# An encoder block with attention and a two-way scan: banks for the scan's copies, an earlier join, and a new order at the start

## The chip, the cores and the metric

The kernel runs on one core of a Trainium2 chip. The metric is device time in microseconds, as the median of several runs: 866.34 us before the change (three runs, 866.20 to 866.93). A profile is one execution of the program, taken on the same core.

The engines are TensorE (PE, with its weight loads as PEld), VectorE (DVE), ScalarE (ACT), GpSimd (POOL) and SyncE (SP). SP issues almost all loads.

## The reference

One layer over 256 tokens of 2048 channels, all in float32. Cut to what matters:

```
h    = rms_norm(x, g_pre)
proj = h @ w_in                        # 2048 x 10688: q_a, kv_a, k_rope | r, k, v, low ranks | z | gates
# branch 1: latent attention, 8 heads
q  = rms_norm(q_a) @ wq_b;  kv = rms_norm(kv_a) @ wkv_b
y1 = softmax((q_nope k_nope + rot(q_rope) rot(k_rope)) * 192**-0.5) v
# branch 2: RWKV-7 in both directions, 16 heads of 64
r, k, v, wd, ad = mix(rin)             # with the mean of both neighbour tokens
w = exp(-exp(-softplus(-(w0 + tanh(wd) @ w2)) - 0.5));  a = sigmoid(a0 + ad @ a2)
kk = k * k_k, normalised per head
for each token:  S = S*w + (S @ -kk) (kk*a)^T + v k^T;   y = S @ r      # forward and backward
y2 = group_norm(y) + bonus * v
merged = sigmoid(g1) * ((y1*silu(z1)) @ w_br_mla) + sigmoid(g2) * ((y2*silu(z2)) @ w_br_rwkv)
x = x + rms_norm(merged @ w_out, g_post)
```

## The kernel before, in words

**Order.** All instructions are written by a planner in Python. Each piece of work is a generator, a stream, that asks for an engine with a cost in us (`yield ("P", 0.48, ready)`), waits for a condition (`"W"`) or for a time (`"T"`). `Streams.run` picks for each engine the stream that can start first, and among near ones the one of lowest rank. Only this choice depends on the costs: the result is one fixed queue per engine, run in order, with semaphores between them. `O.add(stream, rank)` starts a stream. A wrong cost makes a queue whose instructions wait longer than planned.

**Projections.** Weights come in chunks of 4 blocks of 128 channels by 256 columns (`dma_stream`, three raw buffers). `split_stream` splits each into a high part (ScalarE, L331) and a low part (VectorE, L334), and `cm_task` multiplies (L400 to L402): three products per block, high by high, high by low, low by high. These products are the bulk of TensorE's work and fill its queue between all other pieces. Results go to three PSUM banks `d`; all small work uses five banks `m` (`MB`), each 512 float32 wide. `MB.take()` waits for a free one.

**Start.** x arrives in five loads. TensorE transposes the first half of x unscaled (`turned`, tiles `u`) and runs the first half of the low-rank projection on it, to be scaled afterwards (`ev_first`, with the row `R` of 1/rms that `spread` makes: two diagonal tiles on VectorE, four products, one ScalarE copy). `row(t)` sums the squares of token tile t, ScalarE for t = 0 (L1425) and VectorE for t = 1 (L1428), both into one scratch tile `junk`; then comes 1/rms (L1431 to L1435) and the scaling of x (L1442, L1446). The scaled x is transposed again (L1464) and evicted as a high part `hhi` (L1452) and a low part `hlo`, sixteen tiles, k = 8 to 15 first. `start` itself makes derived vectors (`vd`, `ka1`, L1499 to L1503) that `mix` uses as scales.

**RWKV, in quarters.** Four quarters Q of four heads each, and both directions: eight head-directions. `front_k`, `front_d`, `front_v` and `bonus` prepare a quarter, `chunks_of(Q)` does the scan in four chunks of 64 tokens. It makes Gram matrices for all 8 x 4 = 32 chunks (L801), turns the 32 x 32 blocks with VectorE's transposes (L823, L824), inverts 64 triangular blocks of 32 with 60 small VectorE instructions, turns back (L851 to L855), and joins two blocks of 32 to one of 64: two rounds (L856) of 32 small products and four copies (L872), which alternate between ScalarE and VectorE out of one bank. Then the four steps in order (L900): `pu` holds the right-hand sides of all eight head-directions in one bank `mu`, one half of the heads on partitions 0 to 63 and the other on 64 to 127. ScalarE copies one half, VectorE the other (L921, L923); a product with the inverse follows (L928), two copies again (L930, L932), then the products for the next state and the output (L946, L949). The next quarter's preparation starts when `z.u8_free` is set, after the join, and so lies beside the scan. `head_sums` adds over the 64 channels of a head by a product with a block-diagonal matrix `bdr`, from a high and a low part; it is called four times in a quarter.

**Afterwards** come the attention's projections and heads, the two branch projections, and the output projection (L1333 to L1335, 512 columns each).

Of the kernel before, what the change touches and what calls it, by code (L numbers as in the profile page):

```python
# [26 lines left out]
S0 = 1.5  # L27
# [131 lines left out]
def encoder_block_kernel(  # L159
# [117 lines left out]
    def dma_stream():  # L277
        i = 0

        before = {0: [("x", 0, 1)], 1: [("kr", 0, 2)], 2: [("x", 1, 1)], 3: [("kr", 2, 6), ("x", 2, 2)],  # L280
                  5: [("x", 4, 2), ("x", 6, 2)], 6: [("kr", 8, 8)]}
        O.free["S"] = S0
        while True:
            for what, k, n in before.get(i, ()):
                if what == "x":
                    e = yield ("S", 0.73 * n, 0.0)
                    C = slice(256 * k, 256 * (k + n))
                    nc.sync.dma_start(xt[:, :, C], xv[:, :, C])
                    for kp in range(k, k + n):
                        have["xl", kp] = e  # L290
                else:
                    have["kr", k] = yield ("S", 0.182 * n, 0.0)
                    o = krw[k // 8][:, 0:512].rearrange("p (k c) -> p k c", k=8)
                    nc.sync.dma_start(o[:, k % 8:k % 8 + n], w_in_v[:, k:k + n, 1024:1088])
            yield ("W", lambda: i < len(chunks) and i < done["split"] + NRAW)
            c = chunks[i]
            c.t = yield ("S", 0.55 if i < 2 else 1.1 if i < 9 else 1.46, O.free["D"] if i > 9 else 0.0)
            c.load(raws[i % NRAW])
            i += 1
            if i == 8:  # L300
                for t, src in ((rope, rope_d), (bdone, bdone_d), (mask, mask_d), (works[-1], scanm_d)):
                    nc.sync.dma_start(t, src)
            done["dma"] = i
# [117 lines left out]
    def mix(p, m, mcol, o):  # L421

        q = yield from QP.take()
        for j in range(2):
            yield ("A", cA(256, 1))
            act.activation(q[0:m, j, 1:257], p[0:m, j], AF.Copy, scale=vd[0:m, mcol + j:mcol + j + 1])
        t = yield from W.take()
        tv = w2d(t)
        yield ("D", cD(512))
        tt(tv[0:m], q[0:m, :, 0:256], q[0:m, :, 2:258], ALU.add)  # L430
        QP.give(q)
        for j in range(2):
            yield ("D", cD(256))
            stt(o[0:m, j], p[0:m, j], vec[0:m, mcol + j:mcol + j + 1], tv[0:m, j], ALU.mult, ALU.add)
        W.give(t)
# [149 lines left out]
    def head_sums(v, m):  # L585

        n, (hi, lo) = yield from take_r()
        yield from two_parts(v, w2d(hi), w2d(lo))
        yield ("P", 0.476)
        for j in range(2):  # L590
            pe.matmul(p2(m)[:, j], bdr, w2d(hi)[:, j], start=j == 0, stop=False)
            pe.matmul(p2(m)[:, j], bdr, w2d(lo)[:, j], start=False, stop=j == 1)
        give_r(n)
# [69 lines left out]
    def front_d(Q, d):  # L663
# [37 lines left out]
        yield ("D", cD(520))  # L701
# [69 lines left out]
    def chunks_of(Q):  # L771
# [19 lines left out]

        for d in range(2):
# [29 lines left out]
        yield ("D", 4.1)  # L822
        dve.transpose(out=Af[B1], in_=Gu[B1, :, 0:32].rearrange("p u t -> p t u"))  # L823
        dve.transpose(out=Af[B2], in_=Gu[B2, :, 32:64].rearrange("p u t -> p t u"))  # L824
# [4 lines left out]
        yield ("A", cA(1024))  # L829
        act.copy(Af[Lo], Af[Hs])  # L830
        e1 = yield ("D", cD2(512), O.free["D"])
        dve.tensor_copy(Tc[Hs], Ae[Hs, :, 1])
        e0 = yield ("A", cA(512))
# [16 lines left out]
        yield ("D", 2.0)  # L850
        dve.transpose(out=tm[B1].rearrange("p u s -> p s u"), in_=Ai[B1].rearrange("p t s -> p s t"))  # L851
        yield ("D", 2.0)
# [3 lines left out]
        for step in range(2):  # L856

            m = yield from MB.take()
            pm = m[:, 0:256].rearrange("p (u c) -> p u c", u=8)
            e = yield ("P", 0.5, None, "32x32")  # L860
            for u in range(32):
                j = 32 * (u % 4)
                o = pm[j:j + 32, u // 4]
                if step == 0:
                    pe.matmul(o, Gu[B1, u, 32:64], tm[B1, u], start=u < 4, stop=u >= 28, tile_position=(64, j))
                else:
                    pe.matmul(o, tm[B2, u], Gu[B2, u, 32:64], start=u < 4, stop=u >= 28, tile_position=(96, j))
            for j in range(4):
                on, cost = (("A", cA(256) + 0.07), ("D", cD(256) + 0.09))[j % 2]
                yield (on, cost, e)  # L870
                copy = act.copy if on == "A" else dve.tensor_copy
                copy(tm[B2, j::4] if step == 0 else Gu[B1, j::4, 32:64], pm[32 * j:32 * j + 32])  # L872
            MB.give(m)
            yield ("T", max(O.free["A"], O.free["D"]))
# [18 lines left out]
        def by_v(pu, q):  # L893

            for dj in range(4):
                for h in range(2):
                    pe.matmul(pu[R64[1 - h], dj], G[:, 2 * dj + h, q, 0:64], z.uv[q][:, 2 * dj + h], start=dj == 0,
                              stop=(dj == 3 and q == 0))

        for q in range(4):  # L900
# [3 lines left out]
            if q == 0:  # L904
                mu = yield from MB.take()
                pu = mu[:, 0:256].rearrange("p (a c) -> p a c", a=4)
                e = yield ("P", 0.48, None, "128x64")
                by_v(pu, q)
            m = yield from MB.take()
            py = m[:, 0:256].rearrange("p (a c) -> p a c", a=4)  # L910
            if q:
                e = yield ("P", 0.5, None, "64x64")

                for dj in range(4):
                    ar = z.ar[dj // 2][:, dj % 2, q]
                    for h in range(2):
                        pe.matmul(pu[R64[1 - h], dj], ar[R64[h], 0:64], Z[R64[h], dj], start=False, stop=dj == 3)
                    for h in range(2):
                        pe.matmul(py[R64[h], dj], Z[R64[h], dj], ar[R64[h], 64:128], start=dj == 0, stop=False)
            e0 = yield ("A", cA(256) + 0.08, e)  # L920
            act.copy(rhs[Hs, 1], pu[R64[0]])  # L921
            e1 = yield ("D", cD(256) + 0.11, e)
            dve.tensor_copy(rhs[Hs, 0], pu[Hs])  # L923
            e = yield ("P", 0.48, max(e0, e1), "64x64")
            for a in range(4):
                for i in range(2):
                    st = 4 * i + a
                    pe.matmul(pu[R64[i], a], G[Hs, st, q, 0:64], rhs[Hs, st % 2, st // 2], start=a == 0, stop=a == 3)  # L928
            e1 = yield ("A", cA(256) + 0.08, e)
            act.copy(uv[Hs, 0:4], pu[R64[0]])  # L930
            e2 = yield ("D", cD(256) + 0.11, e)
            dve.tensor_copy(uv[Hs, 4:8], pu[Hs])  # L932
            MB.give(mu)
# [4 lines left out]
            mu = (yield from MB.take()) if q < 3 else None  # L938
# [11 lines left out]
            if q < 3:  # L950
                pu = mu[:, 0:256].rearrange("p (a c) -> p a c", a=4)
# [450 lines left out]
    def start():  # L1402
        junk = sb([128, 4, 512], "b8", 1)
# [14 lines left out]
        def row(t):  # L1418
            e = []
# [76 lines left out]
        O.add(spread(), 1)  # L1496
        yield ("W", lambda: ("rs", 1) in have)

# [4 lines left out]
        ts(vd[:, V_KK:V_KK + 8], vec[:, V_KK:V_KK + 8], -1.0, 0.0)  # L1503
        yield ("W", lambda: done["dma"] >= 8)
# [148 lines left out]
```

## Time and profile before

| | before |
|---|---|
| median of three runs | 866.34 us |
| the profiled execution's own time | 866.99 us |
| its span | 865.2 us |
| instructions | 19404 |
| PE busy | 843.4 us (97%) |
| DVE busy | 660.1 us (76%) |
| ACT busy | 501.0 us (58%) |
| POOL busy | 31.8 us (4%) |
| DMA | 139.41 MB, mean 161 GB/s |

The span runs from the first to the last recorded instruction; the execution's own time is a little longer. Matmuls are pipelined: the time shown for one runs over into the next, so how fast products follow one another is read from their starts. A wait is given with the engine and line that ended it.

### The profile page before, as it was taken

What the parts mean: (1) busy time and instruction counts of PE and PEld (TensorE: products, weight loads), DVE (VectorE), ACT (ScalarE), POOL (GpSimd) and SP (SyncE); (2) the same over time, 40 slices, a digit from 0 to 9 for tenths busy, and PEclk for the clock granted to TensorE, in tenths of its full rate; (3) what the DMA queues carried; (4) which work ended last, traced back from release to release, by engine and by line L of the source; (5) the groups of instructions that cost most, each with busy time, mean ns of one, the idle gap of its engine ahead of it and who ended that gap; (6) DMA issues with size and microseconds to landing.
All of it is one profiled execution on the core that took longest, in us unless ns stands there. A gap on an engine that the chain in (4) does not pass through costs nothing.

```text
span 865.2 us, 19404 instructions
## 1 busy us (share of the span) xinstructions
PE 843.4 (97%) x8112; PEld 807.4 (93%) x8112; DVE 660.1 (76%) x1082; ACT 501.0 (58%) x797; POOL 31.8 (4%) x66
## 2 busy tenths in 40 slices
PE   8899999999999999999999999999999999999996
PEld 8899999999999989999999999899999999998884
DVE  5887798869997869887878988766777766765554
ACT  6678654477654587644678444657766543544442
POOL 4210000000000000000010000000000000000000
PEclk9999999999999999999999999999999999999998
DMA  8566646544366624366532566454663575555563
GB/s 273 160 183 169 178 125 183 161 132 123 108 181 185 173 82 117 104 199 178 152 102 77 151 191 174 118 139 159 178 200 112 164 247 191 180 188 193 195 204 113
DMA packets 123528, 139.41 MB, mean 161 GB/s; under 512 B 6704, under 2 KB 110512, under 8 KB 123056
## 3 DMA queue, kind: packets, MB, share of 16 engines
q1 hardware_dynamic: 121664, 135.16, 53.0%
q0 software_dynamic: 768, 1.57, 0.6%
q10 hardware_dynamic: 1008, 1.44, 0.5%
q8 instruction: 63, 1.03, 0.5%
q14 instruction: 25, 0.20, 0.1%
HBM read 136.05 MB, written 2.10 MB: 160 GB/s over the span
## 4 chain that ended last, share of the span: by engine, by line
PE 87%; DVE 7%; ACT 3%; issue 1%; DMA 1%; SPq 0%; POOL 0%; DVEq 0%; ACTq 0%
PE d L400 20%; PE d L402 19%; PE d L401 19%; PE m L1333 2%; PE m L1334 2%; PE m L1335 2%; PE m L801 2%; DVE wlo L334 1%; PE m L402 1%; PE m L400 1%; PE m L401 1%; PE d L1334 1%; PE d L1333 1%; PE d L1335 1%; DVE work L195 1%
## 5 line engine op out<-in xcount | busy, mean ns | idle before, releaser
L331 ACT CAST whi<-raw 128x1024 fp32r<-128x1024 f32 (+3 forms) x252 | 253.1, 1006 | 247.7 <-PE d L401 165.5
L400 PE MATMUL d<-hhi,whi 128*128 128x256 f32 (+1 forms) x1328 | 384.4, 289 | 0.0
L334 DVE TENSOR_TENSOR wlo<-raw,whi 128x1024 fp32r<-128x1024 f32 (+3 forms) x250 | 292.5, 1172 | 116.3 <-ACT whi L331 114.2
L402 PE MATMUL d<-hhi,wlo 128*128 128x256 f32 (+1 forms) x1328 | 375.4, 283 | 1.3 <-DVE wlo L334 1.3
L401 PE MATMUL d<-hlo,whi 128*128 128x256 f32 (+1 forms) x1328 | 375.2, 283 | 0.0
L400 PEld LDWEIGHTS d<-hhi,whi 128*128 128x128 f32 (+1 forms) x1328 | 253.0, 191 | 4.1
L402 PEld LDWEIGHTS d<-hhi,wlo 128*128 128x128 f32 (+1 forms) x1328 | 253.2, 191 | 1.6 <-DVE wlo L334 1.5
L401 PEld LDWEIGHTS d<-hlo,whi 128*128 128x128 f32 (+1 forms) x1328 | 253.4, 191 | 0.1
L195 DVE TENSOR_TENSOR work<-work,work 128x512 f32<-128x512 f32 (+5 forms) x64 | 38.9, 613 | 6.9 <-ACT work L717 2.1
L195 DVE TENSOR_TENSOR u<-u,tmp 128x30 f32<-128x30 f32 (+7 forms) x120 | 29.9, 249 | 3.0
L195 DVE TENSOR_TENSOR tmp<-u 128x30 f32<-128x30 f32 (+7 forms) x120 | 29.8, 249 | 2.7
L402 PE MATMUL d<-uv,wlo 128*128 128x256 f32 x96 | 27.1, 282 | 0.0
L401 PE MATMUL d<-work,whi 128*128 128x256 f32 x96 | 26.9, 280 | 0.0
L400 PE MATMUL d<-uv,whi 128*128 128x256 f32 x96 | 26.8, 279 | 0.0
L1333 PE MATMUL m<-whi,hhi 128*128 128x512 f32 x60 | 23.3, 389 | 0.0
L1334 PE MATMUL m<-wlo,hhi 128*128 128x512 f32 x60 | 23.3, 389 | 0.0
L1335 PE MATMUL m<-whi,hlo 128*128 128x512 f32 x60 | 23.3, 389 | 0.0
L400 PE MATMUL d<-b,whi 128*128 128x256 f32 x80 | 23.0, 288 | 0.0
L402 PE MATMUL d<-b,wlo 128*128 128x256 f32 x80 | 22.6, 282 | 0.0
L401 PE MATMUL d<-ar,whi 128*128 128x256 f32 x80 | 22.4, 280 | 0.0
L195 DVE TENSOR_TENSOR g<-m,mask 128x512 f32<-128x512 f32 x32 | 19.8, 683 | 1.1 <-PE m L801 1.1
L1335 PE MATMUL d<-whi,hlo 128*128 128x512 f32 x48 | 18.7, 389 | 0.0
(331 smaller groups left out, 1451.7 us busy)
## 6 DMA issues: line engine op xcount, KB each, us to landing
raw<-in_w_in_dram SPq DMA_DIRECT2D x160, 512.0 KB, 3.9
raw<-in_w_out_dram SPq DMA_DIRECT2D x32, 512.0 KB, 3.6
raw<-in_w_br_rwkv_dram SPq DMA_DIRECT2D x16, 512.0 KB, 3.4
raw<-in_w_br_mla_dram SPq DMA_DIRECT2D x16, 512.0 KB, 3.4
raw<-in_mla_wkv_b_dram SPq DMA_DIRECT2D x8, 512.0 KB, 3.7
raw<-in_mla_wq_b_dram SPq DMA_DIRECT2D x8, 384.0 KB, 3.5
raw<-in_w_in_dram SPq DMA_DIRECT2D x7, 384.0 KB, 5.3
g<-in_x_dram SPq DMA_DIRECT2D x2, 1024.0 KB, 6.5
```

Of the source, the lines that this page charges most:

```text
L195: dve.tensor_tensor(out=o, in0=a, in1=b, op=op)
L331: act.copy(dst(c.hi), src(raw))
L334: eng.tensor_tensor(out=dst(c.lo), in0=src(raw), in1=dst(c.hi).bitcast(F32), op=ALU.subtract)
L400: pe.matmul(o, hi[:, c:c + m], xhi(k), start=k == k_first and i % 2 == 0, stop=False)
L401: pe.matmul(o, hi[:, c:c + m], xlo(k), start=False, stop=False)
L402: pe.matmul(o, lo[:, c:c + m], xhi(k), start=False, stop=last)
L801: pe.matmul(ms[2 * j + h][:, q * 128:q * 128 + 128], z.kb[R64[h], d, j, q], z.ar[d][R64[h], j, q], start=q == 0, stop=q == 3)
L1333: pe.matmul(banks[t], hhi[:, k, T], hi, start=k == 0, stop=False)
L1334: pe.matmul(banks[t], hhi[:, k, T], lo, start=False, stop=False)
L1335: pe.matmul(banks[t], hlo[:, k, T], hi, start=False, stop=k == KT - 1)
```

## The change

- `head_sums`: two products of 512 columns in place of four of 256.
- The steps of the scan: `pu` is a list of two tiles in two banks, one per half of the heads; all that write or read it follow.
- The join is a function `join(step, ...)`. Its first round becomes a stream of its own, begun behind the first of the three transposes; its four copies all go to ScalarE. The second round uses two banks: two copies on ScalarE from one, two on VectorE from the other.
- The first two transposes (4.1 us as one entry) become two entries, and the copy to the lower partitions one stream behind each (`lower`).
- The start: a scratch tile per token tile (`b8`, `u8`); `spread` has rank 5 for 1; the derived vectors wait for the sixteenth `h` tile, and `mix` waits for them.
- Costs for the planner: `S0`, the loads of the start, the scan instruction L702, the join's copies.

```
@@ start of the loads @@
-S0 = 1.5
+S0 = 1.75
...
-                    e = yield ("S", 0.73 * n, 0.0)
+                    e = yield ("S", 0.8 * n, 0.0)
...
-                    have["kr", k] = yield ("S", 0.182 * n, 0.0)
+                    have["kr", k] = yield ("S", 0.16 * n, 0.0)
...
-            c.t = yield ("S", 0.55 if i < 2 else 1.1 if i < 9 else 1.46, O.free["D"] if i > 9 else 0.0)
+            c.t = yield ("S", 0.65 if i < 2 else 1.1 if i < 9 else 1.46, O.free["D"] if i > 9 else 0.0)
@@ mix @@
+        yield ("W", lambda: "vd" in have)
         q = yield from QP.take()
@@ head_sums @@
-        yield ("P", 0.476)
-        for j in range(2):
-            pe.matmul(p2(m)[:, j], bdr, w2d(hi)[:, j], start=j == 0, stop=False)
-            pe.matmul(p2(m)[:, j], bdr, w2d(lo)[:, j], start=False, stop=j == 1)
+        yield ("P", 0.454)
+        pe.matmul(m, bdr, hi[:, 0:512], start=True, stop=False)
+        pe.matmul(m, bdr, lo[:, 0:512], start=False, stop=True)
@@ front_d @@
-        yield ("D", cD(520))
+        yield ("D", 1.15)
         dve.tensor_tensor_scan(out=fl(th), data0=scanm, data1=fl(lw), initial=0.0, op0=ALU.mult, op1=ALU.add)
@@ chunks_of @@
+        def lower(Af, i):
+            yield ("A", cA(1024))
+            act.copy(Af[32 * i:32 * i + 32], Af[64 + 32 * i:96 + 32 * i])
+            left[0] -= 1
+
+        def join(step, Gu, tm):
+
+            ms = []
+            for _ in range(1 + step):
+                ms.append((yield from MB.take()))
+            pms = [m[:, 0:256].rearrange("p (u c) -> p u c", u=8) for m in ms]
+            e = yield ("P", 0.5, None, "32x32")
+            for u in range(32):
+                j = 32 * (u % 4)
+                o = pms[u % 4 // 2 * step][j:j + 32, u // 4]
+                if step == 0:
+                    pe.matmul(o, Gu[B1, u, 32:64], tm[B1, u], start=u < 4, stop=u >= 28, tile_position=(64, j))
+                else:
+                    pe.matmul(o, tm[B2, u], Gu[B2, u, 32:64], start=u < 4, stop=u >= 28, tile_position=(96, j))
+            for j in range(4):
+                on, cost = (("A", cA(256) + 0.05), ("D", cD(256) + 0.07))[j // 2 * step]
+                yield (on, cost, e if j == 0 or step and j == 2 else O.free[on])
+                copy = act.copy if on == "A" else dve.tensor_copy
+                copy(tm[B2, j::4] if step == 0 else Gu[B1, j::4, 32:64], pms[j // 2 * step][32 * j:32 * j + 32])
+            MB.give(*ms)
+            left[0] -= 1
...
-        yield ("D", 4.1)
-        dve.transpose(out=Af[B1], in_=Gu[B1, :, 0:32].rearrange("p u t -> p t u"))
-        dve.transpose(out=Af[B2], in_=Gu[B2, :, 32:64].rearrange("p u t -> p t u"))
+        for i, (B, o) in enumerate(((B1, 0), (B2, 32))):
+
+            e = yield ("D", 2.05)
+            dve.transpose(out=Af[B], in_=Gu[B, :, o:o + 32].rearrange("p u t -> p t u"))
+            left[0] += 1
+            O.add(lower(Af, i), 0, e)
...
-        yield ("A", cA(1024))
-        act.copy(Af[Lo], Af[Hs])
         e1 = yield ("D", cD2(512), O.free["D"])
         dve.tensor_copy(Tc[Hs], Ae[Hs, :, 1])
+        yield ("W", lambda: left[0] == 0)
+        yield ("T", O.free["A"])
...
-        yield ("D", 2.0)
+        e = yield ("D", 2.0)
         dve.transpose(out=tm[B1].rearrange("p u s -> p s u"), in_=Ai[B1].rearrange("p t s -> p s t"))
+        left[0] += 1
+        O.add(join(0, Gu, tm), 2, e)
         yield ("D", 2.0)
         dve.transpose(out=Gu[B1, :, 0:32].rearrange("p u t -> p t u"), in_=Ai[B1])
         yield ("D", 2.0)
         dve.transpose(out=Gu[B2, :, 32:64].rearrange("p u t -> p t u"), in_=Ai[B2])
-        for step in range(2):
...
+        yield ("W", lambda: left[0] == 0)
+        yield ("T", max(O.free["A"], O.free["D"]))
+        left[0] += 1
+        yield from join(1, Gu, tm)
+        yield ("T", max(O.free["A"], O.free["D"]))
...
-                mu = yield from MB.take()
-                pu = mu[:, 0:256].rearrange("p (a c) -> p a c", a=4)
+                mu = []
+                for _ in range(2):
+                    mu.append((yield from MB.take()))
+                pu = [t[:, 0:256].rearrange("p (a c) -> p a c", a=4) for t in mu]
...
             e0 = yield ("A", cA(256) + 0.08, e)
-            act.copy(rhs[Hs, 1], pu[R64[0]])
+            act.copy(rhs[Hs, 1], pu[0][R64[0]])
             e1 = yield ("D", cD(256) + 0.11, e)
-            dve.tensor_copy(rhs[Hs, 0], pu[Hs])
+            dve.tensor_copy(rhs[Hs, 0], pu[1][Hs])
...
-            act.copy(uv[Hs, 0:4], pu[R64[0]])
+            act.copy(uv[Hs, 0:4], pu[0][R64[0]])
...
-            dve.tensor_copy(uv[Hs, 4:8], pu[Hs])
-            MB.give(mu)
+            dve.tensor_copy(uv[Hs, 4:8], pu[1][Hs])
+            MB.give(*mu)
...
-            mu = (yield from MB.take()) if q < 3 else None
+            mu = []
+            for _ in range(2 if q < 3 else 0):
+                mu.append((yield from MB.take()))
@@ start @@
-        junk = sb([128, 4, 512], "b8", 1)
+        junks = [sb([128, 4, 512], n, 1) for n in ("b8", "u8")]
...
-            e = []
+            e, junk = [], junks[t]
...
-        O.add(spread(), 1)
+        O.add(spread(), 5)
         yield ("W", lambda: ("rs", 1) in have)
+        yield ("W", lambda: ("h", KT - 1) in have)
...
         ts(vd[:, V_KK:V_KK + 8], vec[:, V_KK:V_KK + 8], -1.0, 0.0)
+        have["vd"] = True
```

## Rows read from the trace of the kernel before

**Rows 1.** The page's first part: busy us (share of the span) and instructions.

```profile
PE 843.4 (97%) x8112; PEld 807.4 (93%) x8112; DVE 660.1 (76%) x1082; ACT 501.0 (58%) x797; POOL 31.8 (4%) x66
```

**Rows 2.** Busy time by stretch: from:to, length, busy us of each engine, PEclk, DMA.

```profile
8.00:30.00 22.00, 18.89 (x157) 18.01 (x157) 17.03 (x41) 16.61 (x41) 13.01 (x15) 1.00 0.82 263
30.00:580.00 550.00, 542.76 (x5980) 525.10 (x5978) 456.16 (x762) 331.60 (x513) 17.70 (x41) 1.00 0.53 147
302.00:335.00 33.00, 30.96 (x486) 27.84 (x485) 24.96 (x44) 25.61 (x53) 2.64 (x6) 1.00 0.32 88
426.00:458.00 32.00, 31.10 (x491) 28.41 (x491) 22.72 (x38) 24.34 (x50) 3.22 (x8) 1.00 0.40 113
580.00:856.00 276.00, 275.68 (x1948) 259.10 (x1949) 181.37 (x269) 148.21 (x235) 0.00 (x0) 1.00 0.56 181
856.00:865.20 9.20, 1.15 (x5) 0.57 (x4) 3.69 (x8) 0.98 (x3) 0.00 (x0) 0.76 0.35 124
```

**Rows 3.** TensorE's waits over the run: us in total, times, longest.

```profile
PE m L928 <- DVE work L923: 2.0, 5, 0.7
PE m L1464 <- DVE g L1446: 1.8, 1, 1.8
PE m L592 <- DVE work L195: 1.4, 4, 0.7
PE d L402 <- DVE wlo L334: 1.3, 1, 1.3
PE m L946 <- ACT uv L930: 1.0, 1, 1.0
...
PE m L1464 <- DVE hlo L198: 0.8, 1, 0.8
```

**Rows 4.** TensorE in order of time, 21 to 27 us: start, us, what [idle before].

```profile
21.23 0.28 PE L401 MATMUL d<-hlo,whi 128*128 128x256 f32 x1
...
21.70 0.28 PE L402 MATMUL d<-hhi,wlo 128*128 128x256 f32 x1
23.80 1.31 PE L1464 MATMUL m<-iv,g 128*128 128x128 f32 x10 [1.81 <-DVE g L1446]
...
26.35 0.66 PE L1464 MATMUL m<-iv,g 128*128 128x128 f32 x4 [0.79 <-DVE hlo L198]
```

**Rows 5.** VectorE in order of time, 17 to 24 us.

```profile
17.48 0.84 DVE L1428 SCALAR_TENSOR_TENSOR b<-g 128x512 f32<-128x512 f32 x1 [0.99 <-ACT b L1425]
...
20.74 0.15 DVE L1435 RECIPROCAL rs<-rs 128x1 f32<-128x1 f32 x1
20.82 0.65 DVE L201 TENSOR_SCALAR vd<-iv 128x124 f32<-128x124 f32 x1
...
21.91 1.24 DVE L201 TENSOR_SCALAR work<-iv,rs 128x128 f32<-128x128 f32 x2
23.07 0.67 DVE L1446 TENSOR_SCALAR g<-g,rs 128x512 f32<-128x512 f32 x1
```

**Rows 6.** VectorE's waits, 170 to 585 us: us in total, times, longest.

```profile
DVE work L923 <- ACT work L921: 14.8, 10, 3.3
...
DVE g L872 <- ACT g L872: 1.7, 4, 0.4
```

**Rows 7.** TensorE in order of time at the output projection, 512 columns each.

```profile
779.74 0.39 PE L1333 MATMUL d<-whi,hhi 128*128 128x512 f32 x1
...
781.10 0.39 PE L1333 MATMUL d<-whi,hhi 128*128 128x512 f32 x1
```

**Rows 8.** VectorE in order of time, 355 to 364 us: a transpose and what follows.

```profile
357.78 2.02 DVE L824 STREAM_TRANSPOSE u<-g 32x1024 f32<-32x1024 f32 x1
359.83 2.36 DVE L334 TENSOR_TENSOR wlo<-raw,whi 128x1024 fp32r<-128x1024 f32 x2
```

**Rows 9.** VectorE in order of time in the second quarter's scan.

```profile
312.63 0.43 DVE L923 COPY work<-m 64x256 f32<-64x256 f32 x1 [3.07 <-ACT work L921]
313.09 1.25 DVE L702 TENSOR_TENSOR_SCAN work<-scanm,work 128x520 f32<-128x520 bf16 x1
```

More of the change, by code (lines that the diff above doesn't have):

```diff
@@ L855, in chunks_of @@
         dve.transpose(out=Gu[B2, :, 32:64].rearrange("p u t -> p t u"), in_=Ai[B2])
-        for step in range(2):
[L858 to L874, printed above, removed]
+        yield ("W", lambda: left[0] == 0)
[3 more added lines that the diff above has]
+        yield ("T", max(O.free["A"], O.free["D"]))
         z.u8_free = True
@@ L896, in by_v @@
                 for h in range(2):
-                    pe.matmul(pu[R64[1 - h], dj], G[:, 2 * dj + h, q, 0:64], z.uv[q][:, 2 * dj + h], start=dj == 0,
+                    pe.matmul(pu[1 - h][R64[1 - h], dj], G[:, 2 * dj + h, q, 0:64], z.uv[q][:, 2 * dj + h], start=dj == 0,
                               stop=(dj == 3 and q == 0))
@@ L916, in chunks_of @@
                     for h in range(2):
-                        pe.matmul(pu[R64[1 - h], dj], ar[R64[h], 0:64], Z[R64[h], dj], start=False, stop=dj == 3)
+                        pe.matmul(pu[1 - h][R64[1 - h], dj], ar[R64[h], 0:64], Z[R64[h], dj], start=False, stop=dj == 3)
                     for h in range(2):
@@ L927, in chunks_of @@
                     st = 4 * i + a
-                    pe.matmul(pu[R64[i], a], G[Hs, st, q, 0:64], rhs[Hs, st % 2, st // 2], start=a == 0, stop=a == 3)
+                    pe.matmul(pu[i][R64[i], a], G[Hs, st, q, 0:64], rhs[Hs, st % 2, st // 2], start=a == 0, stop=a == 3)
             e1 = yield ("A", cA(256) + 0.08, e)
-            act.copy(uv[Hs, 0:4], pu[R64[0]])
+            act.copy(uv[Hs, 0:4], pu[0][R64[0]])
             e2 = yield ("D", cD(256) + 0.11, e)
-            dve.tensor_copy(uv[Hs, 4:8], pu[Hs])
-            MB.give(mu)
+            dve.tensor_copy(uv[Hs, 4:8], pu[1][Hs])
+            MB.give(*mu)
             eu = max(e1, e2)
@@ L950, in chunks_of @@
             if q < 3:
-                pu = mu[:, 0:256].rearrange("p (a c) -> p a c", a=4)
+                pu = [t[:, 0:256].rearrange("p (a c) -> p a c", a=4) for t in mu]
                 by_v(pu, q + 1)
```

## The prediction

> **What bounds the kernel now.** I read the page's first part, then the busy time of TensorE by stretch, then what it waited for, and only then the engines it waited for. TensorE is busy for 843.4 of 865.2 us [rows 1]. The 21.8 us that are left lie in five places, found as stretch minus busy time [rows 2]: 3.1 us from 8 to 30, 7.2 us from 30 to 580, where the four quarters of RWKV run, 0.3 us from 580 to 856, 8.1 us at the end, and the rest, 3.1 us, before 8 us, while the first input tile is on its way. The edits do not touch the first and last place; 276 us with 0.3 us of idle say that nothing after the last scan waits for the scan. So 3.1 + 7.2 = 10.3 us are the stock from which waits can be removed, plus what TensorE's own instructions get shorter. Everything else the edits shorten is work beside TensorE, or a chain that TensorE covers with projections, and is worth nothing unless one of those waits hangs on it.
>
> The waits by name [rows 3], where each figure is a sum over the run: 1.8 us of transposes for one scaled piece of x, 0.8 us of transposes for a bank, 2.0 us of the scan's second product (L928) for VectorE's copy L923, 1.0 us of L946 for ScalarE's copy L930, 1.4 us of the head sums for their low part, 1.3 us of one projection for its low part. That is 8.3 of the 10.3 us.
>
> **The change part by part.**
>
> *Start.* TensorE ends the first part of the low-rank projection at 21.7 us and next does something at 23.80 [rows 4], released by VectorE's scaling of x (1.81 us idle), and stands again for 0.79 us before 26.35. VectorE's queue shows why [rows 5]: the second token tile's 1/rms (L1435) is issued at 20.74, then come the derived vectors (L201, from 20.82 to about 22.0) and `spread`'s two diagonal tiles (1.24 us from 21.91), and only then, at 23.07, the scaling that TensorE waits for. The change gives these six instructions a place behind the scaling: the vectors wait until the sixteenth `h` tile exists (the second eight are made first), and `spread` falls from rank 1 to 5. The scaling can then start about 20.9 and end about 21.5, when TensorE's earlier work has just run out: 1.8 us go. The 0.79 us are a wait for a free bank (released by `hlo`, so by an eviction). `spread` holds one of the five `m` banks at that point; later it doesn't: 0.8 us go. What is moved is not dropped: `spread`'s four small products and its one ScalarE copy are issued later, as filler, with no DMA among them; SP's queue keeps its order, and POOL's scalings keep theirs. Behind the moved pieces wait the first eviction of the low-rank task (it needs `R`) and `mix` (it now waits for `vd`); both are needed only when the second half of the low-rank projection ends, 8 blocks of 12 products of 0.1175 us later, 11 us of TensorE work that covers them. If it did not, `spread`'s 1.24 us would come back on TensorE. Next late after this would be the eviction of the first scaled tile. The scratch per token tile removes a wait of VectorE's squares for ScalarE's (0.99 us before the last one [rows 5]); that brings both 1/rms values forward, but TensorE still has projections then, so I give it nothing. Term: 1.81 + 0.79 = 2.6 us; bounds 1.2 (half of it, if the evictions become late at once) and 3.1 (all idle from 8 to 30).
>
> *Head sums.* There are four calls per quarter, sixteen in all, each with four products of 256 columns; now two of 512. The products at 21.23 and 21.70 are four apart, so 256 columns take 0.1175 us start to start [rows 4]; those at 779.74 and 781.10 are six apart, so 512 columns take 0.227 us [rows 7]. Two times 0.1175 less 0.227 is 0.008 us, times 32 pairs 0.3 us, all on TensorE. The first product now also lasts 0.11 us longer before the low part is needed, which takes that much off each of the four waits of L592 (1.4 us [rows 3]): 0.4 us. Term 0.6 us of these 0.7; bounds 0 (the products as long, the low part as late) and 1.4 + 0.3 = 1.7. The page "TensorE: Matmul & The Clock Gate" of the Trainium skill (section "Wait — 56ns, not 53.3ns?") gives a matmul its columns at 2.4 GHz plus 2.5 ns; by that the pairs would save 32 times 2.5 ns, an estimate of 0.1 us, and the rows say 0.3 us with the clock granted in full [rows 2].
>
> *Copies from two banks.* In each of four steps of a scan, ScalarE and VectorE copy one half of the heads each, twice, out of one bank. VectorE's L923 sat idle behind ScalarE's L921 for 14.8 us in ten places, and in the join, where four copies alternate, the waits are as long as the copies [rows 6]. So the order by bank is in the program: two copies, VectorE's of 0.43 us [rows 9], run one after the other although they touch different partitions. With a bank per half each waits only for TensorE. That frees VectorE of up to 14.8 us, but TensorE gets only what it waited: 2.0 us at L928 and 1.0 us at L946 [rows 3]. Not all of this is the bank's: L928 also waits where VectorE was simply late, and the wait at L946 follows the tensor_tensor_scan of 1.25 us [rows 9] that the written-out costs took for 0.62 us (`cD(520)`) and now take for 1.15. I take two thirds, 2.0 us; bounds 0 (the next queue entry is as late) and 3.0.
>
> The section "PSUM bank collisions raise a hardware error" of the page "PSUM — Partial Sum Buffer" of the Trainium skill says guarding is needed by bank and quadrant of 32 partitions, by bank being the simple version; these halves are in different quadrants, so by that rule a second bank would free nothing. The rows of the idle time say that here the program guards by bank.
>
> *The two first transposes apart.* They were one block of 4.1 us, now two of 2.05 with the lowering copies behind each. In the third quarter the block kept a low part of a weight chunk until 359.83 [rows 8] and TensorE lost 1.3 us [rows 3]. Between two blocks the chunk can go first. I take 1.0 us of 1.3; bounds 0 and 1.3. ScalarE pays one more copy over 1024 elements per quarter; at 58% busy [rows 1] it has the room.
>
> *The join begun earlier.* Its products need the first of three transposes of 2 us, and run beside the other two; the copies go to ScalarE alone, then two by two from two banks. The chain of a quarter gets some 2.6 us shorter: four copies of up to 0.43 us, 1.7 us, now lie beside two transposes of 2.0 us [rows 8, 9], and the second four take half their 1.7 us. TensorE has projections throughout, and nothing late in the run waits for the last scan [rows 2]: 0, and what it can bring lies inside the waits counted above.
>
> *Costs that the order is written by.* The load times (`S0`, 0.73 to 0.8, 0.55 to 0.65) add no instruction and move no load on SP, whose order is fixed in the code; they only shift which engine's work comes first in the first 20 us. I give them nothing, and leave them inside the bounds of the start.
>
> *Banks.* A scan step now holds four of five `m` banks where it held three. The next quarter's preparation takes banks one at a time in the same stretch. The trace before has no such wait in a scan; the nearest row is the wait of 0.8 us for a bank at the start [rows 3]. I set 0.5 us against the gain; bounds 0 and the slower rival below.
>
> *Sum.* 2.6 + 0.6 + 2.0 + 1.0 - 0.5 = 5.7 us. The profiled execution took 866.99 us, a span of 865.2 and 1.8 around it: 861.3 by its own time. It lay 0.65 us above the median of the three runs, so for the median 866.34 - 5.7 = **860.6 us**.
>
> **The rivals.**
>
> *Only the start pays* (863.4 us). The scan's waits change places: VectorE's queue is as full, and the next instruction on it is late instead. For it: at L928 some of VectorE's copies had no idle time before them, they stood in a queue. Against it: 14.8 us of idle in that very queue [rows 6]. Time: 866.34 - 2.6 - 0.3.
>
> *The bank is not what orders the copies* (862.6 us): the change doesn't do what it says, the 2.0 us stay, and no bank pays for anything. 866.34 - 5.7 + 2.0. Against it: copies in different quadrants that alternate strictly. The page "PSUM — Partial Sum Buffer" of the Trainium skill, in the section named above, speaks for it.
>
> *No change* (866.2 us): the moved vectors and `spread` land where TensorE needs the queue next, and the new order of the whole program gives back the rest; the waits from 30 to 580 are spread unevenly, 2.0 us in one scan and 0.9 in the next [rows 2], with the same code, so an order can be that much better or worse by chance.
>
> *Slower: too few banks* (872.7 us). While a scan holds four banks, the next quarter's preparation needs six takes (four for the two directions' decay and rate, one for the key's norm, one for the bonus). Three quarters are prepared beside a scan: 18 takes. TensorE's queue is in order, so a product whose bank is still being read holds up the projections behind it. At the price of the longest wait at L928, 0.7 us [rows 3], 18 cost 12.6 us against gains of 6.2: +6.4. It decides from the ninth such wait on. Against it: the order is written out with the banks counted, so a product is placed where its bank is expected free; only what runs later than planned can wait.
>
> **How the numbers follow.** Forecast 0.55, start alone 0.20, order not by bank 0.07, no change 0.10, too few banks 0.08. The forecast's own range is 857.2 (the upper bounds 3.1 + 1.7 + 3.0 + 1.3 = 9.1) to 863.1 (start and head sums alone, 3.2). The range of 857.0 to 866.0 holds nearly all of it, the two smaller gains and half of no change: 0.82. A measurement of this kernel tells 0.2% (1.7 us) from no change. Faster than that: the forecast, 0.85 of the start alone, and the order not by bank, less a little at the edge: 0.78. Same: 0.12. Slower: 0.10.
>
> **What would show it.** Start: TensorE without the gap at 21.7 us, and the L201 group behind the last `hlo`. If the gap stands with another releaser, the term is wrong. Copies: VectorE's idle time behind ScalarE at L923 near zero, both copies starting together, and the waits of L928 and L946 halved; copies apart as before mean the bank was not it. Join: four ScalarE copies beside two transposes. Head sums: 32 products of 512 columns, 0.227 us apart. Transposes: a chunk's low part between the two. Too few banks: waits of L688, L591 or the scan's own products for an eviction, above all in the second to fourth quarter. The forecast is wrong if TensorE's idle time from 30 to 580 does not fall under 5 us.

## The result: 857.4 us, and the profile after

The changed kernel takes 857.38 us in the median (857.10 to 858.01, four runs) against 866.27 us before: a ratio of 0.990, 95% interval 0.988 to 0.992. The forecast was 860.6 us, a gain of 5.7; the gain is 8.9 us. The profiled execution took 857.24 us with a span of 855.5. Four executions of the kernels compared below took 934 to 1633 us, among them the only profiled one of the early join with the old copies; medians leave them out, and no wait is read from that trace.

The page's first part after, to be read against [rows 1]:

```profile
PE 840.8 (98%) x8080; PEld 804.8 (94%) x8080; DVE 656.8 (77%) x1074; ACT 508.3 (59%) x809; POOL 31.3 (4%) x66
```

The first, second and late stretch after, against [rows 2] (stretch, length, busy us of PE, PEld, DVE, ACT, POOL, PEclk, DMA; the late stretch ends 10 us earlier):

```profile
8.00:30.00 22.00, 20.45 (x171) 19.59 (x170) 18.95 (x45) 18.28 (x46) 12.66 (x15) 1.00 0.86 276
30.00:580.00 550.00, 546.66 (x6008) 528.62 (x6008) 461.73 (x766) 347.97 (x536) 17.39 (x41) 1.00 0.53 149
580.00:846.00 266.00, 265.32 (x1867) 249.05 (x1866) 170.62 (x253) 137.15 (x218) 0.00 (x0) 1.00 0.56 182
```

TensorE's idle time falls from 3.1 to 1.6 us between 8 and 30, and from 7.2 to 3.3 us between 30 and 580; late in the run it changes little, from 0.3 to 0.7. Over the span it falls from 21.8 to 14.7 us, by 7.1, but the span is 9.7 us shorter. The rest lies in the busy time, and most of it can be waits that don't show as idle: a product of 256 columns is shown for 0.28 us but starts 0.12 us behind its predecessor, so up to 0.16 us of each wait is covered by shown work. Starts tell more. Counted in order, the 1053rd projection product starts at 154.9 us before and at 152.8 after, the last of 4800 at 769.4 and at 759.7: some 2 us are gained before 155 us and 7.6 between there and 770, where most of the work of the four quarters lies. The 2 us hold luck too: TensorE waited 2.0 us for x in the profiled execution before, and not at all in the one after.

TensorE's waits after (us in total, times, longest), against [rows 3]:

```profile
PE m L837 <- DVE g L195: 1.7, 3, 1.1
...
PE d L401 <- DVE hlo L198: 0.7, 1, 0.7
PE m L1486 <- ACT g L1464: 0.7, 1, 0.7
...
PE m L937 <- DVE z L195: 0.4, 2, 0.2
PE m L592 <- DVE work L195: 0.4, 2, 0.2
```

The scan's waits (L928 and L946, now L948 and L968), the bank wait and the 1.8 us for the scaling (L1446, now L1468) are gone; the head sums keep 0.4 of 1.4 us. No wait in a scan is for an eviction that holds a bank, so the slower rival, too few banks, did not happen. One wait for a bank grew, behind the scans: at L837 TensorE transposes into a bank that VectorE frees by masking a Gram matrix, 1.7 us at 219.6, 335.1 and 458.5 us. Before, the same wait was

```profile
PE m L810 <- DVE g L195: 0.5, 1, 0.5
```

New are, at the start, 0.7 us each for a piece of x from ScalarE and for the first low part `hlo`.

VectorE's waits from 160 to 585 us, against [rows 6]:

```profile
DVE uv L952 <- PE m L948: 6.3, 6, 1.8
DVE work L943 <- PE m L937: 6.1, 4, 1.9
```

The copies L923 (now L943) wait for TensorE alone, and the join's copies (L872, now L815) for no other engine's copy at all.

### The profile page after: what moved, and what is told of

It is laid out like the page before. It is cut to its first block, busy times and chain, and to the rows that moved or that the text cites. A ratio compares the mean times of both kernels' runs of the same rounds, so it can differ in the third digit from the quotient of the medians.

```text
span 855.5 us, 19366 instructions
## 1 busy us (share of the span) xinstructions
PE 840.8 (98%) x8080; PEld 804.8 (94%) x8080; DVE 656.8 (77%) x1074; ACT 508.3 (59%) x809; POOL 31.3 (4%) x66
## 4 chain that ended last, share of the span: by engine, by line
PE 86%; DVE 8%; ACT 3%; DMA 1%; issue 1%; SPq 0%; DVEq 0%; ACTq 0%
PE d L400 19%; PE d L401 18%; PE d L402 18%; PE m L1357 2%; PE m L1356 2%; PE m L1355 2%; DVE wlo L334 2%; PE m L828 2%; DVE work L195 1%; PE d L1357 1%; PE d L1356 1%; PE d L1355 1%; PE m L402 1%; PE m L400 1%; PE m L401 1%
## 5 line engine op out<-in xcount | busy, mean ns | idle before, releaser
L400 PE MATMUL d<-b,whi 128*128 128x256 f32 x96 | 27.5, 287 | 0.0
L402 PE MATMUL d<-b,wlo 128*128 128x256 f32 x96 | 27.1, 282 | 0.0
L401 PE MATMUL d<-ar,whi 128*128 128x256 f32 x96 | 26.9, 280 | 0.0
L1355 PE MATMUL d<-whi,hhi 128*128 128x512 f32 x48 | 18.7, 389 | 0.0
```

The costliest lines, as they stand in the source:

```text
L400: pe.matmul(o, hi[:, c:c + m], xhi(k), start=k == k_first and i % 2 == 0, stop=False)
L401: pe.matmul(o, hi[:, c:c + m], xlo(k), start=False, stop=False)
L402: pe.matmul(o, lo[:, c:c + m], xhi(k), start=False, stop=last)
L1355: pe.matmul(banks[t], hhi[:, k, T], hi, start=k == 0, stop=False)
```

## The experiments

Times are medians. The intervals of the ratios are 1.5 to 3 us wide from end to end, so a difference below about 1 us is not told by time alone; there I also compare starts of the same projection product. One thing disturbs that: when x arrives. Kernels with the same first instructions wait between 0 and 1.7 us for it. Where a kernel is called slower than the changed one, all its executions lie above the slowest of the changed one's (858.01 us).

### One bank for both halves

```
-                pu = [t[:, 0:256].rearrange("p (a c) -> p a c", a=4) for t in mu]
+                pu = [mu[0][:, 0:256].rearrange("p (a c) -> p a c", a=4)] * 2
```

> The kernel after, with both halves of the heads in the first of the two banks again; the second bank is still taken and left empty, so every engine's queue keeps its order. Theory 'the bank orders the copies': VectorE's copies L943 and L952 wait for ScalarE's again, by some 10 us in sum, and 2 to 5 us of the time come back: 859.4 to 862.4 us. Rival 'the copies' order never cost TensorE anything, the new order of the queues is what gained': within 0.5 us of the kernel after, 857.4 us, with the waits between the copies back all the same.

859.05 us, ratio 0.991 (0.990 to 0.993): 1.7 us slower than the changed kernel. Every queue has the same order as in it, so this is the bank alone. VectorE's waits, 160 to 585 us, with one bank:

```profile
DVE work L943 <- ACT work L941: 12.8, 8, 3.0
DVE uv L952 <- ACT uv L950: 8.6, 6, 2.4
```

and TensorE's:

```profile
PE m L948 <- DVE work L943: 1.7, 4, 0.6
```

One pair of copies, ScalarE and then VectorE, with one bank:

```profile
302.94 0.36 ACT L941 COPY work<-m 64x256 f32<-64x256 f32 x1
```

```profile
303.34 0.43 DVE L943 COPY work<-m 64x256 f32<-64x256 f32 x1 [2.90 <-ACT work L941]
```

and the same pair in the changed kernel:

```profile
302.53 0.36 ACT L941 COPY work<-m 64x256 f32<-64x256 f32 x1
```

```profile
301.88 0.43 DVE L943 COPY work<-m 64x256 f32<-64x256 f32 x1 [1.86 <-PE m L937]
```

ScalarE is late there with other work; with one bank VectorE stands behind it. The term of 2.0 us nearly held, and it shows as the prediction said: with one bank VectorE idles 9.0 us longer in front of these copies (21.4 for 12.4), and TensorE waits 1.7 us for them. The wait of 1.0 us for ScalarE's copy (L946 before) does not come back, so that one went with the new order and not with the bank. The Trainium skill ("PSUM — Partial Sum Buffer", section "PSUM bank collisions raise a hardware error") asks for a guard by bank and quadrant, and these halves lie in different quadrants. The trace shows that this program orders the copies by the bank alone; whether a finer guard would do is not tried.

### The start: load costs, place of the vectors, all of it

In the changed kernel, the old costs of the loads:

```
-S0 = 1.75
+S0 = 1.5
...
-                    e = yield ("S", 0.8 * n, 0.0)
+                    e = yield ("S", 0.73 * n, 0.0)
```

> The kernel after, with the load costs of before (S0 1.5, 0.73, 0.182, 0.55); the queues differ from the kernel after only in the first 25 us. Theory of the prediction 'load costs add and move nothing': 857.4 us, within 0.5. Rival 'the load costs put the first low-rank products ahead of the second pair of transposes': TensorE idles about 2 us more before 8 us, and 1.0 to 2.0 us come back: 858.4 to 859.4 us.

858.41 us, ratio 0.991 (0.989 to 0.992), 1.0 us slower by the medians; products lag by 1.0 us at the 25th and 1.5 from the 109th on, and a part of this can be x, for which this execution waited 1.6 us and the changed kernel's not at all. The instructions are the same; what the costs change is whose turn comes first. With the old costs the first projections stand behind the second transposes of x, as in the kernel before:

```profile
5.01 1.06 PE L1413 MATMUL m<-ones 128*128 128x128 f32 x8
8.06 0.66 PE L1464 MATMUL m<-iv,g 128*128 128x128 f32 x4 [1.99 <-DMA g<-in_x_dram]
8.47 0.36 PE L400 MATMUL d<-hhi,whi 128*96 128x256 f32 x1
```

and after, where they no longer stand behind these transposes and their load:

```profile
5.93 1.16 PE L1435 MATMUL m<-ones 128*128 128x128 f32 x6
6.85 0.36 PE L400 MATMUL d<-hhi,whi 128*96 128x256 f32 x1
```

In the changed kernel, the derived vectors and `spread` in their old place:

```
-        O.add(spread(), 5)
+        O.add(spread(), 1)
...
-        yield ("W", lambda: ("h", KT - 1) in have)
```

> The kernel after, with the derived vectors and spread in their old place (rank 1, no wait for the sixteenth tile). Theory of the prediction: the gap of about 2 us at 19 to 22 us and the one for a bank are back, 2.6 us: 860.0 us. Rival 'only part of that gap was this': the kernel after still has 1.6 us of idle time at that place, so 1.0 us comes back: 858.4 us.

857.45 us, ratio 0.989 (0.988 to 0.991): nothing. Then the kernel before with all edits of the start (costs, place, scratch) and none of the others:

```
-S0 = 1.5
+S0 = 1.75
...
-        junk = sb([128, 4, 512], "b8", 1)
+        junks = [sb([128, 4, 512], n, 1) for n in ("b8", "u8")]
...
-        O.add(spread(), 1)
+        O.add(spread(), 5)
```

> The kernel before, with the edits of the start alone (load costs, place of the derived vectors and of spread, a scratch per token tile). Theory of the prediction: 2.6 us, 863.7 us. Rival 'the start is worth its first 40 us in the trace of the kernel after': 2.35 us there, of which some 0.7 came from an early load in that one execution, so 1.6 us, 864.7 us. What the new order of the rest brings or takes comes on top, 2 us either way.

864.07 us, ratio 0.998 (0.997 to 0.999): 1.7 us less by the medians and 2.1 by the ratio than the executions of the kernel before taken beside it, while the scan's waits stay as they were. At last the kernel before with the place alone:

```
-        O.add(spread(), 1)
+        O.add(spread(), 5)
...
+        yield ("W", lambda: ("h", KT - 1) in have)
```

> The kernel before with one edit: the accumulator of the head totals and the spread scales get their place in the program directly behind the norm chain, as in the changed kernel; loads keep their old costs. My theory of the start (the term of 2.6 us in the prediction): the time falls by about 2.6 us, to 863.7 us, and the scale on VectorE starts right behind the square root's reciprocal. Rival: the first low part and the evictions of the projections stand in front of the next product anyway and take up what is won, as placing it back in the changed kernel (0.07 us) suggests: 866.0 us, within 0.5 us of before.

864.86 us, ratio 0.9985 (0.9976 to 0.9994): 1.5 us by the medians (1.3 by the ratio), not 2.6. TensorE in this kernel, against [rows 4]:

```profile
21.32 1.31 PE L1465 MATMUL m<-iv,g 128*128 128x128 f32 x10 [0.17 <-DVE g L1447]
22.47 0.61 PE L1487 MATMUL m<-work,ones 128*128 128x128 f32 x4
...
24.53 0.36 PE L401 MATMUL d<-hlo,whi 128*96 128x256 f32 x1 [1.06 <-DVE hlo L198]
```

and VectorE, against [rows 5]:

```profile
19.99 0.65 DVE L201 TENSOR_SCALAR work<-iv,rs 128x128 f32<-128x128 f32 x1
20.55 0.72 DVE L1447 TENSOR_SCALAR g<-g,rs 128x512 f32<-128x512 f32 x1
21.19 0.73 DVE L201 TENSOR_SCALAR work<-iv,rs 128x128 f32<-128x128 f32 x1
21.82 2.25 DVE L334 TENSOR_TENSOR wlo<-raw,whi 128x768 fp32r<-128x768 f32 x2
24.00 2.43 DVE L198 SCALAR_TENSOR_TENSOR hlo<-m,iv,hhi 128x256 fp32r<-128x256 f32 x6
```

Both waits go as planned (1.81 to 0.17, 0.79 to none), and a new one of 1.06 us comes: the first `hlo` stands behind two low parts. 2.6 - 0.17 - 1.06 = 1.4 us, about what was measured. So the scaling was early, and the eviction next late. Not all six instructions moved: one of `spread`'s two tiles still stands in front of the scaling (19.99). The place is worth 1.5 us in the order of before and nothing in that of after: edits of one start stand in for each other and don't add.

### The join as before, its beginning, its copies

The whole old join in the changed kernel: begun behind the third transpose, one bank, copies alternating (both diffs below, together).

> The kernel after, with the join as before: begun behind the third transpose, both rounds out of one bank with copies alternating between ScalarE and VectorE. Theory 'the join is a chain beside TensorE's work': the scans start about 2.6 us later each, TensorE's idle time stays, 857.4 us within 1. Rival 'a shorter join takes waits off the whole middle part, because VectorE stands in its queue for each of the alternating copies': 2 to 4 us come back, 859.4 to 861.4 us.

859.20 us, ratio 0.992 (0.991 to 0.994): 1.8 us slower. The two parts by themselves: first the late beginning with the new copies,

```
+        yield ("D", 2.0)
+        dve.transpose(out=Gu[B1, :, 0:32].rearrange("p u t -> p t u"), in_=Ai[B1])
+        e = yield ("D", 2.0)
+        dve.transpose(out=Gu[B2, :, 32:64].rearrange("p u t -> p t u"), in_=Ai[B2])
         left[0] += 1
         O.add(join(0, Gu, tm), 2, e)
-        yield ("D", 2.0)
...
```

> The changed kernel with the first round of the join begun behind the third transpose again; its copies stay as in the changed kernel. It parts the 1.8 us that the whole old join costs. If the early begin is what counts: 858.5 to 859.2 us, and a new wait of the second join product for its copy. If the copies (bank and engine) count: 857.4 us, within 0.3 us of the changed kernel.

856.56 us, ratio 0.989 (0.988 to 0.990): not slower, by the medians 0.8 us faster than the changed kernel, which the overlapping intervals don't establish. Then the early beginning with the old copies:

```
-            for _ in range(1 + step):
+            for _ in range(1):
...
-                on, cost = (("A", cA(256) + 0.05), ("D", cD(256) + 0.07))[j // 2 * step]
+                on, cost = (("A", cA(256) + 0.07), ("D", cD(256) + 0.09))[j % 2]
```

> The changed kernel with the join begun early, but both its parts in one bank and the copies alternating between ScalarE and VectorE as before. The complement of the late begin: if the copies count, 858.5 to 859.2 us; if the early begin counts, 857.4 us, within 0.3 us. If both cost about 0.9 us each, the two parts add; if each costs nothing alone, the begin and the copies stand in for each other.

858.80 us, ratio 0.991 (0.990 to 0.993): 1.4 us slower, most of the old join's 1.8. So in this order the copies count, and the early beginning is not seen to earn anything. What the copies of the old join waited for, over the run:

```profile
  DVE u L815: 5.6, 4
  ACT g L815: 3.2, 4
  DVE g L815: 2.4, 4
  ACT u L815: 1.7, 4
  PE m L808: 1.4, 3
```

and with the late beginning and the new copies:

```profile
  PE m L810: 3.1, 3
  PE m L808: 2.9, 3
```

12.9 us in which ScalarE and VectorE stood behind each other's copies are gone, and so are VectorE's two copies in the first round of each quarter. With the old join TensorE itself waits for the last of them:

```profile
PE m L810 <- DVE u L815: 0.4, 2, 0.2
```

As idle time little of it shows. From the first product of the second round to the next projection product it takes 1.04, 1.04, 1.14 and 1.11 us in the four quarters, against 0.68 in each with the late beginning and the new copies: 1.6 us in sum, so most of what the old join costs here is TensorE standing at products of the join. The kernel before has the same copies, with 3.6 + 3.4 + 1.7 + 1.5 = 10.2 us of such idle time, but there the second round takes 0.77 us once and 0.68 three times. The old copies' price belongs to the new order; that taking them away is a part of the gain over the kernel before is not shown. Which of the two, bank or engine, carries the difference is open: no run parted them. What the early join with the old copies loses its 1.4 us to is open too.

### The two transposes in one block

```
+        e = yield ("D", 4.1)
+
         for i, (B, o) in enumerate(((B1, 0), (B2, 32))):
-
-            e = yield ("D", 2.05)
```

> The kernel after, with the first two transposes as one entry of 4.1 us again (the two lowering copies stay). Theory of the prediction: one low part of a weight chunk is caught behind a block in one of four quarters and TensorE loses 1.0 to 1.3 us: 858.5 us. Rival 'that wait was chance': 857.4 us, within 0.5, and no wait of L402 for L334 in the trace.

858.94 us, ratio 0.992 (0.990 to 0.993): 1.55 us slower. TensorE's first wait in the list, with the block:

```profile
PE d L402 <- DVE wlo L334: 2.7, 2, 1.4
```

It is 1.4 us at 236.2 and again at 357.0; the bank wait at L837 falls from 1.7 to 0.3 in the same kernel, which takes off a part of the price. VectorE with the block, second quarter:

```profile
230.82 4.10 DVE L852 STREAM_TRANSPOSE u<-g 32x1024 f32<-32x1024 f32 x2
234.95 2.36 DVE L334 TENSOR_TENSOR wlo<-raw,whi 128x1024 fp32r<-128x1024 f32 x2
```

and in the changed kernel, where a weight chunk's low part stands between the two:

```profile
229.66 2.03 DVE L852 STREAM_TRANSPOSE u<-g 32x1024 f32<-32x1024 f32 x1
231.73 0.48 DVE L198 SCALAR_TENSOR_TENSOR work<-d,iv,work 128x256 f32<-128x256 f32 x1
232.13 1.22 DVE L334 TENSOR_TENSOR wlo<-raw,whi 128x1024 fp32r<-128x1024 f32 x1
...
233.75 2.03 DVE L852 STREAM_TRANSPOSE u<-g 32x1024 f32<-32x1024 f32 x1
```

### Head sums of 256 columns; the scan instruction's old cost

```
-        pe.matmul(m, bdr, hi[:, 0:512], start=True, stop=False)
-        pe.matmul(m, bdr, lo[:, 0:512], start=False, stop=True)
+        for j, t, f, g in ((0, hi, True, False), (0, lo, False, False), (1, hi, False, False), (1, lo, False, True)):
+            pe.matmul(p2(m)[:, j], bdr, w2d(t)[:, j], start=f, stop=g)
```

> The kernel after, with the head sums as four products of 256 columns, high and low part in turn, at the cost of two of 512; every queue keeps its order. Theory of the prediction: 0.3 us for the products and up to 0.11 us more in each wait for a low part: 857.4 + 0.6 = 858.0 us. Rival 'the products cost the same either way': 857.4 us.

857.35 us, ratio 0.990 (0.989 to 0.992): no difference. Two products of 512 columns in the changed kernel:

```profile
296.74 0.40 PE L591 MATMUL m<-work,bdr 128*128 128x512 f32 x1
296.98 0.40 PE L592 MATMUL m<-work,bdr 128*128 128x512 f32 x1
```

The next product starts 0.23 us behind the second. Where nothing waits, a head sum takes 0.46 us from its first product to the one behind it, and with four products 0.47: 0.2 us in all sixteen, too little to see. The waits for the low part stay at 0.6 us with four products (0.4 after, 1.4 before), so most of them went with the new order and not with the wider products.

```
-        yield ("D", 1.15)
+        yield ("D", cD(520))
```

> The kernel after, with the scan instruction L702 planned at cD(520), 0.62 us, in place of 1.15. Theory 'wrong costs make the waits of the scans': the instructions behind L702 come late again, TensorE waits 1 us more in sum in the four scans: 858.4 us. Rival 'this cost gains nothing': 857.4 us, within 0.5. Since all queues change from 70 us on, a difference of less than 1 us is not told from chance.

857.41 us, ratio 0.989 (0.988 to 0.991): no difference, though this cost alone makes another order. The 1 us of waits that was expected in the scans did not come back.

### A version meant to be better

```
             c = chunks[i]
+            if i == 7: yield ("W", lambda: ("h", 9) in have)
```

> A version meant to beat both: the changed kernel, with the low part of the last x chunk held back in the plan until the first normalised high part has been split, so that one low part instead of two stands in front of it on VectorE. If the wait of TensorE for the first low part of the normalised rows (about 1.1 us at 23 to 24 us) is on the path: about 0.7 us less, 856.7 us. Rival: the low part held back is late for its own projection products, or the plan behind it shifts: 857.4 us or up to 1 us more.

857.34 us, ratio 0.990 (0.989 to 0.992): no gain. One low part fewer stands in front of the first `hlo`, and TensorE's wait for it is gone, though transposes now wait 0.5 us for an eviction; products run 0.4 us ahead of the changed kernel's up to 155 us. At the head sums at 215 us, whose two parts come from ScalarE and VectorE at nearly the old time, the lead shrinks to 0.04, and the last product starts 0.07 us behind the changed kernel's. What is won at the start is taken back where TensorE waits for something that did not get earlier. Of all the kernels, the changed one with the late beginning of the join is the fastest by its median, 856.56 us.

## Why the prediction was right, and where it was not

The direction, the place (start and the quarters) and the range held. The size did not: 5.7 us forecast, 8.9 measured. The range held narrowly: 857.38 us is 0.4 us inside its lower end, and the gain is nearly the sum of all upper bounds (9.1 us), though the terms that single edits show make little more than half of it. That the total fell inside owes something to luck. Term by term:

- **Start, 2.6 us.** All edits of the start together gave 1.7 to 2.1 us, so the size held in part, but the step behind it did not. The two waits it counted did go; the price of "next late after this would be the eviction of the first scaled tile" was left out of the sum, and was 1.06 us. On the other side stands "I give them nothing" for the load costs: in the order of after, taking them back costs 1.0 us.
- **Head sums, 0.6 us.** Measured 0. The width of the products saves 0.2 us by their starts, and the waits for the low part differ by another 0.2 us at most (0.6 to 0.4).
- **Two banks, 2.0 us.** Measured 1.7, with VectorE's wait and the one of L928 where they were expected; the one of L946 went by another way. The rival that the bank doesn't order the copies is refuted.
- **Transposes apart, 1.0 us.** Measured 1.55. The wait came back twice, at 1.4 us each, where the trace before had it once at 1.3.
- **Join, 0.** In the new order the old copies cost 1.4 to 1.8 us. "TensorE has projections throughout" leaves out that TensorE makes the join's own products: its queue is in order, and where the second round comes up before the last copy is done, the projections behind it wait as well, 1.6 us in sum. In the kernel before that cost 0.1 us, so a gain of 0 over it is not refuted. The length of the join's chain indeed doesn't matter: the late beginning costs nothing.
- **Banks, -0.5 us.** No such wait appears in a scan. The bank wait that grew (L837, 0.5 to 1.7 us) lies behind the scans, which have given their banks back by then; it is 0.3 us with the transposes in one block, so it moves with the order.

The terms that single edits show, start 1.7 to 2.1, banks 1.7 and transposes 1.55 us, make 5.0 to 5.4 of the 8.9 us, if they add at all, and each difference is uncertain by about 1 us. The remaining 3.5 to 3.9 us are not parted by edits; they include whatever the new copies of the join bring, and the joint order that all edits make. The two traces show where TensorE got time back, not by which edit. An estimate from them, for 30 to 600 us: from the start of each product I take off the distance that the same pair of products keeps where it is shortest (the lowest tenth), and sum what is left by line. In all some 7 us less are lost: 2.3 at the head sums, 1.6 at the projections that wait for a low part, 1.5 at L928, 1.3 at L946, 0.8 at L1022, against 1.2 more at L837, 0.8 more at L652 and 0.4 more at L937. The join's products lose the same in both, 3.6 and 3.5 us. The test that the prediction set for itself, idle time below 5 us between 30 and 580, came out at 3.3.

## What to carry to other kernels

A chain beside the bound engine is free only as long as the bound engine takes no part in it: with the old copies TensorE stood 0.36 to 0.46 us at the join's second round in each quarter, although projections were left to do behind it. When a stall is removed, look for the next instruction that the same consumer needs, and put its own queue's delay into the sum at once. Undo edits one at a time in the new kernel and also add them one at a time to the old: an edit worth 1.5 us in one order was worth nothing in the other.

## What the hardware showed that was not expected

VectorE's low part over 768 columns takes 1.33 us in the kernel before and 0.96 us in the changed one:

```profile
19.49 1.33 DVE L334 TENSOR_TENSOR wlo<-raw,whi 128x768 fp32r<-128x768 f32 x1
```

```profile
18.78 0.96 DVE L334 TENSOR_TENSOR wlo<-raw,whi 128x768 fp32r<-128x768 f32 x1
```

Before, GpSimd scaled x beside it:

```profile
19.03 2.36 POOL L1446 TENSOR_SCALAR g<-g,rs 128x512 f32<-128x512 f32 x2 [0.39 <-DVE rs L1435]
```

After, GpSimd ran nothing from 18.04 to 19.64 and began scaling at 20.08. Other kernels go the same way: a low part that starts while GpSimd scales takes 1.33 us with the place alone and 1.32 with the old costs, and one without it 0.96 with the old place. It can also hit the other side: at 23.66 us in the kernel before the low part takes 0.95 us beside a scaling, and GpSimd's instruction 1.64 where it takes 0.69 alone. The Trainium skill ("SBUF — State Buffer", section "SBUF: two separate sides") says that a VectorE instruction with two inputs in SBUF and a GpSimd instruction that reads SBUF exclude each other, and that the later one waits until the first has ended. The traces agree in direction, and the 0.95 us that GpSimd loses at 23.66 are the length of the low part; no run here changed this alone.
